# mLSTM scores from fp32r parts instead of fp32, and the second parts of three weight pieces made on GpSimd

## The chip, the cores and the metric

The kernel runs on one core of a Trainium2 chip. The metric is device time in microseconds (us) of one execution: the median of three runs before the change is 978.38 us.

## The reference, cut to what matters

Two post-norm layers: half-step SwiGLU FFN, token mixing, half-step SwiGLU FFN, each followed by a LayerNorm, on 256 positions of width 1024. The mixer of the second layer is an mLSTM of four heads of width 192 beside a cross-attention into 256 memory tokens. Of the mLSTM the part that matters here is:

```python
qk = jax.nn.silu(causal_dwconv(qk, qk_conv_w))     # width 4, over positions
q, k = jnp.split(qk, 2, -1)                        # 768 = 4 heads x 192 each
...
sc = jnp.einsum('bhtd,bhsd->bhts', q_, k_) * w_intra
num = (jnp.einsum('bhts,bhse->bhte', sc, v_) + ...)
den = jnp.sum(sc, -1) + ...
h = num / jnp.maximum(jnp.abs(den), jnp.exp(-m_t))[..., None]
```

The kernel computes the chunked recurrence as one causal 256 x 256 matrix of scores for each head, weighted by a decay matrix. Everything is asked for in fp32.

## The kernel before, in words

**Exact parts.** An fp32 value x is split into h, x rounded to fp32r, and l = x - h, also fp32r. `split` (L107) does it: ScalarE (ACT) copies into h (L108), VectorE (DVE) subtracts (L109). A product of two values is then three fp32r matmuls: h by h, h by l, l by h. Nearly all matmuls of the kernel are such products; a few are in plain fp32, among them the mLSTM scores and the sums over values (`numer`).

**Weights.** The weights are listed as pieces in the order of their use (`pieces`), each 1 MB or less. `trace_piece` (L118) loads a piece into a `raw` tile (three buffers) by a DMA on the queue of SP (L138) and splits it, 1024 columns at a time, into `wh` and `wl` (five buffers each). `get` (L146) runs one piece ahead of use. A raw buffer is free for the next DMA when both parts have been made from it, and a wh and wl buffer when the matmuls have read it. The dictionary `behind` puts a piece's split, on the engine concerned, behind a given instruction.

The pieces of the mLSTM stage are, in order of use (their number follows in the names of the order's rows): wm 0 (122) for the queries of the cross-attention; wv 0,0 and 0,1 (123, 124) for the values of heads 0 and 1; wm 1 (125), wm 4 (126), wm 2 (127), wm 5 (128); wv 1,0 and 1,1 (129, 130) for the values of heads 2 and 3; wm 3 (131), wm 6 (132); four pieces of the output projection (133 to 136); then the gate and up weights of the last FFN (137 on). wm 1 to 3 make k, wm 4 to 6 make q, 256 channels each.

**The mLSTM stage**, `mlstm_mixer`, in the order in which TensorE (PE) runs it from L809 on. `qk_piece` (L718) projects 256 channels (tiles qkp, two banks of 128 channels, 24 products each, L457 to L459), applies the convolution from the bank (one ACT and three DVE instructions for each 128 channels, L724 and L726) into a tile qr, and then the SiLU of 512 columns on ACT (L730) into a tile `qk`. Names such as qr01 mean which = 0 (q; 1 is k) and i = 1. PE does k0 and q0 (i = 0), with the cross-attention's scores between them; in the middle of q0 come the matmuls `negm` that spread a row over the partitions, from which DVE (L708) and ACT (L709, L711) make the four decay matrices, in buffers named kT, vm, og and decay (`decay`, L698). Then k1 with the transposes pT of the softmax in its middle (L520), q1, the values of heads 2 and 3 (tile v), the outputs of the cross-attention (xo, L530), the scores of heads 0 and 1 (`mscores(0)`, tiles ms), k2 with `numer` in its middle, q2, the first parts of the output projection (yo), the scores of heads 2 and 3 (`mscores(1)`), and the rest.

**mscores** (L735). The 768 channels lie in six chunks of 128 partitions. Each head has one whole chunk (`al`) and half of another (`lo` or `hi`, 64 partitions), by the table HP. For each of two row tiles of positions (256 columns, then 128, because of the causal triangle) it does the whole chunks, as two matmuls of 64 output columns each (`mm_halves`, L209), then the half chunks (L746), one head's beside the other's.

**Banks.** PSUM has two rings of four banks. The ring of `ybank` holds, in this stage and in this order: the scores of the cross-attention (4), negm of heads 0 and 1, negm of heads 2 and 3, pT (4), v (2), xo (2), ms of heads 0 and 1. So the fourth pT takes the bank of the second negm.

**Order.** The instructions of each engine stand in a fixed order that a scheduler makes from the program when it is built; an engine runs them in that order.

Of the kernel before, what the change touches and what calls it, by code (L numbers as in the profile page):

```python
# [8 lines left out]
F32 = mybir.dt.float32  # L9
F32R = mybir.dt.float32r  # L10
AF = mybir.ActivationFunctionType
# [3 lines left out]
P = 128  # L15
T = 256
# [15 lines left out]
def trunk(ctx: ExitStack, tc: tile.TileContext, d, out):  # L32
    nc = tc.nc
    pe, act, dve, pool = nc.tensor, nc.scalar, nc.vector, nc.gpsimd
# [5 lines left out]
    hp = ctx.enter_context(tc.tile_pool(name="hp", bufs=5))  # L40
# [7 lines left out]
    def ybank(name):  # L48
        return psy.tile([P, 512], F32, tag="y", name=name)
# [45 lines left out]

    state = {"next": 0, "used": 0}
    made = {}
    behind = {}

    def after(*ins):  # L100

        stack = ExitStack()
        for i in ins:
            stack.enter_context(tc.issue_after(i))
        return stack

    def split(raw, h, l):  # L107
        act.activation(h, raw, AF.Copy)  # L108
        dve.tensor_sub(l, raw, h.bitcast(F32))  # L109

    def new_act(name):

        return actp.tile([P, KC, 2, T], F32R, tag="a", name=name)

    def split_act(raw, a, k0, n):
        split(raw.rearrange("p (k t) -> p k t", k=n), a[:, k0:k0 + n, 0], a[:, k0:k0 + n, 1])

    def trace_piece(first=False):  # L118
        n = state["next"]
        if n >= len(pieces):  # L120
            return
        key, src, width = pieces[n]
        state["next"] = n + 1
        if not first:
            raw = rawp.tile([P, 2048], F32, tag="raw", name=f"raw{n}")
        if key == ("mem",):
            nc.sync.dma_start(raw, src)
            made[key] = new_act("memT")
            for q in range(2):
                split_act(raw[:, 1024 * q:1024 * q + 1024], made[key], 4 * q, 4)  # L130
            return
        h = wp.tile([P, 2048], F32R, tag="wh", name=f"wh{n}")
        l = wp.tile([P, 2048], F32R, tag="wl", name=f"wl{n}")
        made[key] = (h, l)
        if first:
            return h, l
        if n >= 6:
            nc.sync.dma_start(raw[:, :width], src)  # L138
        for c in range(0, width, SPLIT):
            s = slice(c, min(c + SPLIT, width))  # L140
            if n < 6:
                nc.sync.dma_start(raw[:, s], src[:, s])
            with after(*behind.get(key, ())):
                split(raw[:, s], h[:, s], l[:, s])

    def get(*key):  # L146
        while state["next"] < len(pieces) and state["next"] <= state["used"] + 1:
# [12 lines left out]
    first = [trace_piece(first=True) for _ in range(2)]  # L160
# [7 lines left out]
    for k in range(KC):  # L168
        q, o = (k, 0) if k < 2 else (1 + k // 2, k % 2 * CH)
        nc.sync.dma_start(xw[q][:, o:o + CH], d["xw"][:, k * CH:(k + 1) * CH])  # L170
        h, l = first[k // 4]
        s = slice((k % 4) * 512, (k % 4) * 512 + 512)
# [33 lines left out]
    def mm_halves(o, a, b, start, stop):  # L206

        for m in HALVES:
            pe.matmul(o[m], a[:, m], b, start=start, stop=stop)  # L209

    def tsl(t):
        return slice(t * P, (t + 1) * P)
# [397 lines left out]
    lo, hi, al = slice(0, 64), slice(64, 128), slice(0, 128)  # L610
    HP = [((0, al), (1, lo)), ((1, hi), (2, al)), ((3, al), (4, lo)), ((4, hi), (5, al))]

    def mlstm_mixer(mix, i):
# [7 lines left out]
        for t in range(2):  # L621
            banks = [ybank(f"op{t}{h}") for h in range(2)]
            for k in range(KC):
                for h in range(2):
                    n = 392 if h else 384
                    s = slice((k % 2) * 776 + 384 * h, (k % 2) * 776 + 384 * h + n)
# [21 lines left out]
        li, f, e, u = [rows[0][:NH, n, :] for n in range(4)]  # L648
# [6 lines left out]
        mask = kv[0][:, 384:]  # L655
# [42 lines left out]
        def decay():  # L698
            nb = {h: ybank(f"negm{h}") for h in (0, 2)}
            o = [nb[h // 2 * 2][:, h % 2 * T:h % 2 * T + T] for h in range(NH)]  # L700
            for h in range(NH):
                for n in range(2):
                    pe.matmul(o[h], pick[:, h:h + 1].to_broadcast([P, P]), eh[:, n], start=n == 0,
                              stop=n == 1)
            for h in range(NH):
                Et = E[h]
                for t in range(2):
                    m = dve.tensor_add(Et[:, 256 * t:256 * t + P], o[h][:, tsl(t)], mask)  # L708
                    act.activation(Et[:, 256 * t:256 * t + P], Et[:, 256 * t:256 * t + P], AF.Exp,  # L709
                                   bias=cols[:, t, h:h + 1])  # L710
                last = act.activation(Et[:, P:256], o[h][:, P:], AF.Exp, bias=cols[:, 0, h:h + 1])  # L711
            behind["wm", 5] = behind["wv", 1, 0] = (m.ins,)
            return last.ins


        qk = [hp.tile([P, 2, 2, T], F32, tag="h", name=f"qk{n}") for n in range(3)]

        def qk_piece(which, i, mid=None):  # L718
            r = tmp(f"qr{which}{i}")

            def use(c, b):
                o = c * 256
                w = [qcw[:, 6 * which + 2 * i + c, q:q + 1] for q in range(4)]
                act.activation(r[:, o:o + 256], b, AF.Copy, scale=w[3])  # L724
                for q, sh in ((0, 3), (1, 2), (2, 1)):
                    dve.scalar_tensor_tensor(r[:, o + sh:o + 256], b[:, :256 - sh], w[q],  # L726
                                             r[:, o + sh:o + 256], op0=ALU.mult, op1=ALU.add)

            proj_direct(get("wm", (1 if which else 4) + i), f"qkp{which}{i}", use, mid)
            return lambda: act.activation(qk[i][:, which].rearrange("p c t -> p (c t)"), r, AF.Silu)  # L730

        def qkc(c, which, r, s):
            return qk[c // 2][r, which, c % 2, s]

        def mscores(a):  # L735
            hs = (2 * a, 2 * a + 1)
            b = {h: (ybank if a == 0 else mbank)(f"ms{h}") for h in hs}
            for s in range(2):
                ts_ = slice(0, 256) if s == 0 else slice(P, 256)
                o = {h: b[h][:, 0:256] if s == 0 else b[h][:, 256:384] for h in hs}  # L740
                for h in hs:
                    c = next(c for c, r in HP[h] if r is al)
                    mm_halves(o[h], qkc(c, 1, al, tsl(s)), qkc(c, 0, al, ts_), True, False)
                for h in hs:
                    c, r = next((c, r) for c, r in HP[h] if r is not al)
                    pe.matmul(o[h], qkc(c, 1, r, tsl(s)), qkc(c, 0, r, ts_), start=False, stop=True)  # L746
            for h in hs:
                dve.scalar_tensor_tensor(E[h][:, :384], b[h][:, :384], DH ** -0.5, E[h][:, :384],
                                         op0=ALU.mult, op1=ALU.mult)
# [66 lines left out]
        ends = []  # L816
# [9 lines left out]
        xa.values(1)  # L826
        mscores(0)
        qk_piece(1, 2, lambda: (numer(0, 0), numer(1, 0)))()
        qk_piece(0, 2)()
        o = OutProj(1, mix, i)  # L830
        tokens(0, 0)
        tokens(1, 0)
# [25 lines left out]
    mix = new_act("mix0")  # L858
# [11 lines left out]
    o = OutProj(0, mix, 1)  # L870
# [63 lines left out]
```

## Time and profile before

| what | value |
|---|---|
| median of 3 runs | 978.38 us (978.30 to 978.86) |
| the profiled execution, whole | 978.59 us |
| its span, first to last instruction | 976.2 us |
| granted clock of TensorE, mean | 0.999 |
| the mLSTM stage from k0 to the end of the second scores | about 700 to 764 us of the span |
| GpSimd (POOL) busy, over the span | 20.5 us in 32 instructions |
| HBM read | 185.01 MB |

The profile is of one execution. A row of its timeline gives the start in us from the span's start, the duration, the engine, the line of the kernel, the operation, out<-in, the shapes, and how many like instructions in a row it stands for; PE is a matmul, PEld the load of its weights. A matmul's recorded duration includes its way through the array, so the pace of matmuls is read from start to start, not from durations. A plain fp32 matmul of the program shows as two records, an fp32r matmul as one. Where idle time stood before an instruction, the row ends with it and with what ended it; "issue" means that nothing in the profile held it.

### The profile page before, as it was taken

What the parts mean: (1) busy time and instruction counts of PE and PEld (TensorE: products, weight loads), DVE (VectorE), ACT (ScalarE), POOL (GpSimd) and SP (SyncE); (2) the same over time, 40 slices, a digit from 0 to 9 for tenths busy, and PEclk for the clock granted to TensorE, in tenths of its full rate; (3) what the DMA queues carried; (4) which work ended last, traced back from release to release, by engine and by line L of the source; (5) the groups of instructions that cost most, each with busy time, mean ns of one, the idle gap of its engine ahead of it and who ended that gap; (6) DMA issues with size and microseconds to landing.
All of it is one profiled execution on the core that took longest, in us unless ns stands there. A gap on an engine that the chain in (4) does not pass through costs nothing.

```text
span 976.2 us, 13253 instructions
## 1 busy us (share of the span) xinstructions
PE 967.2 (99%) x5266; PEld 831.0 (85%) x5266; DVE 662.9 (68%) x1016; ACT 527.1 (54%) x847; POOL 20.5 (2%) x32
## 2 busy tenths in 40 slices
PE   9999999999999999999999999999999999999997
PEld 8888888888888888888888888889999788888885
DVE  7685657869667755656875656568698786565565
ACT  7565555447535545555444555545885345555540
POOL 0000000000000000000000000001000000000000
PEclk9999999999999999999999999999999999999999
DMA  9784645566444654646375464633645446546421
GB/s 327 282 305 165 218 170 207 178 224 216 168 173 176 241 200 160 218 170 214 131 278 196 151 234 139 233 124 108 237 148 215 167 175 246 202 147 226 159 87 43
DMA packets 28142, 186.91 MB, mean 191 GB/s; under 512 B 3505, under 2 KB 3505, under 8 KB 7217
## 3 DMA queue, kind: packets, MB, share of 16 engines
q1 hardware_dynamic: 27792, 185.55, 52.6%
q8 instruction: 41, 0.67, 0.3%
q10 hardware_dynamic: 288, 0.52, 0.1%
q14 instruction: 21, 0.16, 0.0%
HBM read 185.01 MB, written 1.05 MB: 191 GB/s over the span
## 4 chain that ended last, share of the span: by engine, by line
PE 97%; DMA 1%; DVE 1%; ACT 0%; issue 0%; SPq 0%; DVEq 0%; ACTq 0%
PE gu L197 43%; PE y L189 8%; PE y L191 8%; PE y L190 8%; PE gx L191 2%; PE gx L189 2%; PE gx L190 2%; PE cx L197 2%; PE cb L197 2%; PE cg L197 2%; PE yo L189 2%; PE yo L191 2%; PE yo L190 1%; PE qkp L457 1%; PE qkp L458 1%; PE qkp L459 1%
## 5 line engine op out<-in xcount | busy, mean ns | idle before, releaser
L109 DVE TENSOR_TENSOR wl<-raw,wh 128x1024 fp32r<-128x1024 f32 x334 | 394.2, 1206 | 139.9 <-ACT wh L108 139.0
L108 ACT ACTIVATE wh<-raw 128x1024 fp32r<-128x1024 f32 x334 | 333.0, 1043 | 125.3 <-PE y L191 63.2
L197 PE MATMUL gu<-x,wh 128*128 128x512 f32 x1216 | 388.9, 395 | 0.2
L197 PEld LDWEIGHTS gu<-x,wl 128*128 128x128 f32 x1216 | 228.3, 188 | 52.2 <-DVE wl L109 0.8
L197 PE MATMUL gu<-x,wl 128*128 128x256 f32 x1216 | 242.8, 278 | 0.3 <-DVE wl L109 0.2
L197 PEld LDWEIGHTS gu<-x,wh 128*128 128x128 f32 x1216 | 189.5, 189 | 4.0 <-ACT wh L108 0.6
L189 PE MATMUL y<-wh,h 128*128 128x512 f32 (+1 forms) x352 | 137.4, 390 | 0.0
L190 PE MATMUL y<-wl,h 128*128 128x512 f32 (+1 forms) x352 | 136.6, 388 | 0.0
L191 PE MATMUL y<-wh,h 128*128 128x512 f32 (+1 forms) x352 | 136.5, 389 | 0.0
L202 DVE TENSOR_TENSOR s<-s,gu 128x256 f32<-128x256 f32 x152 | 63.0, 417 | 103.8 <-ACT s L201 103.6
L201 ACT ACTIVATE s<-gu 128x256 f32<-128x256 f32 x152 | 57.9, 382 | 105.7 <-PE gu L197 105.7
L191 PEld LDWEIGHTS y<-wh,h 128*128 128x128 f32 x352 | 66.1, 188 | 14.2 <-DVE h L334 0.4
L190 PEld LDWEIGHTS y<-wl,h 128*128 128x128 f32 x352 | 66.1, 188 | 13.6
L189 PEld LDWEIGHTS y<-wh,h 128*128 128x128 f32 x352 | 66.1, 188 | 12.9 <-ACT h L333 0.7
L333 ACT ACTIVATE h<-s 128x256 fp32r<-128x256 f32 x76 | 31.8, 418 | 66.1 <-DVE s L330 66.1
L329 ACT ACTIVATE s<-s 128x256 f32<-128x256 f32 x76 | 31.6, 416 | 37.6 <-DVE s L202 37.6
L334 DVE TENSOR_TENSOR h<-s,h 128x256 fp32r<-128x256 f32 x76 | 32.0, 421 | 17.3 <-ACT h L333 17.1
L189 PE MATMUL gx<-wh,x 128*128 128x512 f32 x96 | 38.0, 396 | 0.0
L191 PE MATMUL gx<-wh,x 128*128 128x512 f32 x96 | 37.6, 392 | 0.0
L190 PE MATMUL gx<-wl,x 128*128 128x512 f32 x96 | 37.4, 390 | 0.0
L330 DVE SCALAR_TENSOR_TENSOR s<-s 128x256 f32<-128x256 f32 x76 | 32.0, 421 | 1.7 <-ACT s L329 0.4
L457 PE MATMUL qkp<-x,wh 128*128 128x256 f32 x96 | 27.5, 287 | 0.0
(223 smaller groups left out, 967.6 us busy)
## 6 DMA issues: line engine op xcount, KB each, us to landing
raw<-in_wgu SPq DMA_DIRECT2D x83, 1024.0 KB, 4.8
raw<-in_wd SPq DMA_DIRECT2D x43, 1024.0 KB, 4.8
raw<-in_wconv SPq DMA_DIRECT2D x10, 1024.0 KB, 4.8
raw<-in_wout SPq DMA_DIRECT2D x8, 1024.0 KB, 4.8
raw<-in_wm SPq DMA_DIRECT2D x7, 1024.0 KB, 5.0
gb<-in_lngb SPq DMA_DIRECT2D x6, 1024.0 KB, 4.6
raw<-in_wkv SPq DMA_DIRECT2D x4, 1024.0 KB, 4.9
raw<-in_wop SPq DMA_DIRECT2D x4, 776.0 KB, 4.3
```

Of the source, the lines that this page charges most:

```text
L108: act.activation(h, raw, AF.Copy)
L109: dve.tensor_sub(l, raw, h.bitcast(F32))
L189: pe.matmul(o, ah, bh, start=start, stop=False)
L190: pe.matmul(o, ah, bl, start=False, stop=False)
L191: pe.matmul(o, al, bh, start=False, stop=stop)
L197: pe.matmul(o, w[part], b, start=(k, part) == (0, 0), stop=(k, part) == (KC - 1, 0))
L201: act.activation(o, bank[:, T:], AF.Copy)
L202: dve.tensor_add(o, o, bank[:, :T])
L330: dve.scalar_tensor_tensor(t_[:, 256:], t_[:, :256], 0.5, t_[:, 256:], op0=ALU.mult, op1=ALU.mult)
L333: act.activation(hh, t_[:, 256:], AF.Copy)
L334: dve.tensor_sub(hT[g][:, 1, fc, :], t_[:, 256:], hh.bitcast(F32))
L457: pe.matmul(o, w[0][:, s], a[:, 0], start=k == 0, stop=False)
```

## The change

The scores take q and k as exact parts. After the SiLU, which now writes back into qr, each 128 channels are split by `split` into h and l. The parts of chunks 0 to 2 go into the tile `mix`, the mixer's output, whose first six chunks receive no outputs before those scores are done; those of chunks 3 to 5 go into three tiles that take the place of `qk`. `mscores` does each product as three fp32r matmuls, the whole chunks with all 128 output columns at once, the half chunks alternating between the two heads.

The second parts of the pieces wm 5, wv 1,0 and wv 1,1 are subtracted on POOL instead of DVE, and no longer wait for the last addition of `decay`. The split of the first gate piece of the last FFN is put behind the split of q2.

```diff
+    aside = {("wm", 5), ("wv", 1, 0), ("wv", 1, 1)}
...
-    def split(raw, h, l):
-        act.activation(h, raw, AF.Copy)
-        dve.tensor_sub(l, raw, h.bitcast(F32))
+    def split(raw, h, l, eng=None):
+        first = act.activation(h, raw, AF.Copy).ins
+        return first, (eng or dve).tensor_sub(l, raw, h.bitcast(F32)).ins
...
-                split(raw[:, s], h[:, s], l[:, s])
+                split(raw[:, s], h[:, s], l[:, s], pool if key in aside else None)
...
-            behind["wm", 5] = behind["wv", 1, 0] = (m.ins,)
...
-        qk = [hp.tile([P, 2, 2, T], F32, tag="h", name=f"qk{n}") for n in range(3)]
+        late_qk = [hp.tile([P, 2, 2, T], F32R, tag="h", name=f"qk{n}") for n in range(3)]
+
+        def qk(c, which):
+            return mix[:, 2 * c + which] if c < 3 else late_qk[c - 3][:, which]
...
-            return lambda: act.activation(qk[i][:, which].rearrange("p c t -> p (c t)"), r, AF.Silu)
+            def done():
+                act.activation(r, r, AF.Silu)
+                for c in range(2):
+                    o = qk(2 * i + c, which)
+                    ends = split(r[:, c * T:(c + 1) * T], o[:, 0], o[:, 1])
+                return ends
+            return done
...
+                def products(h, whole, n):
+                    c, r = next((c, r) for c, r in HP[h] if (r is al) == whole)
+                    k, q = ((0, 0), (0, 1), (1, 0))[n]
+                    pe.matmul(o[h], qk(c, 1)[r, k, tsl(s)], qk(c, 0)[r, q, ts_],
+                              start=whole and n == 0, stop=not whole and n == 2)
                 for h in hs:
-                    c = next(c for c, r in HP[h] if r is al)
-                    mm_halves(o[h], qkc(c, 1, al, tsl(s)), qkc(c, 0, al, ts_), True, False)
-                for h in hs:
-                    c, r = next((c, r) for c, r in HP[h] if r is not al)
-                    pe.matmul(o[h], qkc(c, 1, r, tsl(s)), qkc(c, 0, r, ts_), start=False, stop=True)
+                    for n in range(3):
+                        products(h, True, n)
+                for n in range(3):
+                    for h in hs:
+                        products(h, False, n)
...
-        qk_piece(0, 2)()
+        behind["gu", 1, 1, 0, 0] = qk_piece(0, 2)()
```

The change adds lines, so a line of the changed kernel has a number higher by one in the upper part (L108 is L109 there). Three places in the order of the instructions show what moves. The first is ACT while the decay matrices are made, before the change; wh131 is the first part of wm 3, og and decay the last two decay matrices, negm2 the bank that they are read from:

```order
L709 ACTIVATE og_5796<-og_5796,cols_5867 128x128
L724 ACTIVATE qr00_6140<-qkp00_1_6208,qcw_169 128x256
L709 ACTIVATE vm0_1750<-vm0_1750,cols_5867 128x128 x2
L711 ACTIVATE vm0_1750<-negm0_6178,cols_5867 128x128
L711 ACTIVATE og_5796<-negm2_6179,cols_5867 128x128
L709 ACTIVATE decay3_5862<-decay3_5862,cols_5867 128x128 x2
L711 ACTIVATE decay3_5862<-negm2_6179,cols_5867 128x128
L730 ACT_TABLE_LOAD
```

The same place on ACT now:

```order
L109 ACTIVATE wh131_6424<-raw131_6423 128x1024
L710 ACTIVATE vm0_1750<-vm0_1750,cols_5867 128x128 x2
L712 ACTIVATE vm0_1750<-negm0_6178,cols_5867 128x128
L710 ACTIVATE og_5796<-og_5796,cols_5867 128x128
L712 ACTIVATE og_5796<-negm2_6179,cols_5867 128x128
L728 ACTIVATE qr00_6140<-qkp00_1_6208,qcw_169 128x256
L109 ACTIVATE wh131_6424<-raw131_6423 128x1024
L710 ACTIVATE decay3_5862<-decay3_5862,cols_5867 128x128 x2
L712 ACTIVATE decay3_5862<-negm2_6179,cols_5867 128x128
L736 ACT_TABLE_LOAD
```

Both halves of wh131, which stood behind the SiLU of k0 and q0, now stand ahead of the last decay matrix.

The second place is PE in the middle of k1, where the four softmax tiles are transposed. Before:

```order
L520 MATMUL pT1_10_6289<-ident_162,p1_10_6114 128x128 x4
L520 MATMUL pT1_11_6295<-ident_162,p1_11_6124 128x128 x4
L457 MATMUL qkp11_1_6301<-x3_5553,wh127_6142 128x256
L458 MATMUL qkp11_1_6301<-x3_5553,wh127_6142 128x256
L459 MATMUL qkp11_1_6301<-x3_5553,wl127_6143 128x256
```

And now:

```order
L521 MATMUL pT1_10_6297<-ident_162,p1_10_6114 128x128 x4
L458 MATMUL qkp11_1_6309<-x3_5553,wh127_6142 128x256
L459 MATMUL qkp11_1_6309<-x3_5553,wh127_6142 128x256
L460 MATMUL qkp11_1_6309<-x3_5553,wl127_6143 128x256
L521 MATMUL pT1_11_6303<-ident_162,p1_11_6124 128x128 x4
```

Three products of k1 have moved ahead of the fourth group of transposes.

The third place is PE at the first scores, which follow the cross-attention's outputs xo and read the tile qk before:

```order
L530 MATMUL xo1_1_6474<-p1_11_6124,vm1_1752 64x256 x2
L209 MATMUL ms0_6481<-qk0_5869 64x256 x2
L209 MATMUL ms1_6482<-qk1_5870 64x256 x2
L746 MATMUL ms0_6481<-qk0_5869 128x256
L746 MATMUL ms1_6482<-qk0_5869 128x256
```

And now the tile mix:

```order
L531 MATMUL xo1_1_6490<-p1_11_6124,vm1_1752 64x256 x2
L753 MATMUL ms0_6497<-mix1_5696 128x256 x3
L753 MATMUL ms1_6498<-mix1_5696 128x256 x3
L753 MATMUL ms0_6497<-mix1_5696 128x256
L753 MATMUL ms1_6498<-mix1_5696 128x256
```

Six fp32 matmuls, each two records in the profile, have become twelve of fp32r, since the last two rows come three times; then both repeat all of it with 128 columns.

More of the change, by code (lines that the diff above doesn't have):

```diff
@@ L707, in decay @@
                 for t in range(2):
-                    m = dve.tensor_add(Et[:, 256 * t:256 * t + P], o[h][:, tsl(t)], mask)
+                    dve.tensor_add(Et[:, 256 * t:256 * t + P], o[h][:, tsl(t)], mask)
                     act.activation(Et[:, 256 * t:256 * t + P], Et[:, 256 * t:256 * t + P], AF.Exp,
@@ L729, in qk_piece @@
             proj_direct(get("wm", (1 if which else 4) + i), f"qkp{which}{i}", use, mid)
-            return lambda: act.activation(qk[i][:, which].rearrange("p c t -> p (c t)"), r, AF.Silu)
-        def qkc(c, which, r, s):
-            return qk[c // 2][r, which, c % 2, s]
+            def done():
[5 more added lines that the diff above has]
+            return done
         def mscores(a):
```

## The prediction

> **What bounds the kernel now.** I read the page first, then who waited on PE's weight side in the stage that the change touches, then PE's timeline around the two score groups. The page:
>
> ```profile
> PE 967.2 (99%) x5266; PEld 831.0 (85%) x5266; DVE 662.9 (68%) x1016; ACT 527.1 (54%) x847; POOL 20.5 (2%) x32
> PE 97%; DMA 1%; DVE 1%; ACT 0%; issue 0%; SPq 0%; DVEq 0%; ACTq 0%
> ```
>
> PE is busy for 99% of the span and carries 97% of the chain that ended last. Whether that holds in this stage too, the waits of PE's weight loads between 690 and 782 us say (longest first; these are the first four):
>
> ```profile
> PEld ms L746 <- issue: 1.1, 4, 0.4
> PEld ms L209 <- issue: 1.0, 3, 0.4
> PEld num L209 <- issue: 0.4, 1, 0.4
> PEld cols L691 <- DVE qr L726: 0.3, 1, 0.3
> ```
>
> The largest wait for another engine is 0.3 us. So relieving DVE can return almost nothing; the time changes by what PE itself gains or loses, and by waits that are new.
>
> **The scores' own time.** PE's timeline, first score group, then the products of k2 that follow:
>
> ```profile
> 738.62 1.08 PE L209 MATMUL ms<-qk 128*64 128x256 f32 x8
> 739.63 0.70 PE L746 MATMUL ms<-qk 64*128 64x256 f32 x4
> 740.26 0.66 PE L209 MATMUL ms<-qk 128*64 128x128 f32 x8
> 740.85 0.49 PE L746 MATMUL ms<-qk 64*128 64x128 f32 x4
> 741.27 0.39 PE L457 MATMUL qkp<-x,wh 128*128 128x256 f32 x1
> 741.49 0.28 PE L458 MATMUL qkp<-x,wh 128*128 128x256 f32 x1
> 741.61 0.28 PE L459 MATMUL qkp<-x,wl 128*128 128x256 f32 x1
> ```
>
> Second group, between products of the output projection:
>
> ```profile
> 761.08 0.39 PE L191 MATMUL yo<-wh,mix 128*128 128x512 f32 x1
> 761.39 1.08 PE L209 MATMUL ms<-qk 128*64 128x256 f32 x8
> 762.41 0.70 PE L746 MATMUL ms<-qk 64*128 64x256 f32 x4
> 763.04 0.66 PE L209 MATMUL ms<-qk 128*64 128x128 f32 x8
> 763.63 0.49 PE L746 MATMUL ms<-qk 64*128 64x128 f32 x4
> 764.05 0.50 PE L189 MATMUL yo<-wh,mix 128*128 128x512 f32 x1
> 764.39 0.39 PE L190 MATMUL yo<-wl,mix 128*128 128x512 f32 x1
> 764.62 0.39 PE L191 MATMUL yo<-wh,mix 128*128 128x512 f32 x1
> ```
>
> Start to start, the four L746 records take 0.63 us with 256 columns and 0.42 with 128. They run as two pairs, one head's half chunk beside the other's, so the 0.21 us between them is 2 x 128 columns: 0.82 ns a column in fp32, and 0.21 us is left that does not depend on the columns. That is the price of changing the shape in which the array is used (64*128, 128*64, 128*128) and of the first weights. The eight L209 records (four pairs of 64 output columns) give the same: 1.02 in the second group against 0.59 is 0.84 ns a column, with 0.16 us left.
>
> An fp32r product of 256 columns takes 0.12 us (741.49 to 741.61), one of 512 columns 0.23 (764.39 to 764.62): 0.43 ns a column, half the fp32 pace, and an fp32r product is one record where fp32 needs two. On paper that is 3 x 0.43 = 1.3 ns a column for three products against 2 x 0.83 = 1.7. But each product loads its weights anew:
>
> ```profile
> 741.27 0.19 PEld L457 LDWEIGHTS qkp<-x,wh 128*128 128x128 f32 x1
> 741.38 0.19 PEld L458 LDWEIGHTS qkp<-x,wh 128*128 128x128 f32 x1
> ```
>
> Two loads of 128 columns with nothing in front start 0.11 us apart. At 256 moving columns the load is just hidden; at 128 it should set the pace.
>
> **The sum for PE.** Each group becomes 24 records, as before: six whole products of 256 columns, three pairs of half ones, six of 128 columns, three pairs. I take 0.12 us a slot for all 18: 2.16 us, plus 0.21 for each change of shape.
>
> - First group: it follows 64-column matmuls, so there are five changes (the last to k2): 2.16 + 1.05 = 3.21. Before, from 738.62 to full pace (741.49 less 0.12), 2.75. So +0.46.
> - Second group: the products in front have its shape, so four changes: 2.16 + 0.84 = 3.00. Before, from 761.08 + 0.23 to 764.39 - 0.23, 2.85. So +0.15.
>
> Together +0.6. The uncertain price is the 18 slots of 128 columns, since no fp32r matmul under 256 columns is in this trace. From below, the line through 0.12 and 0.23 gives 0.07 a slot, so 18 x 0.05 = 0.9 less, in sum -0.3. From above, the fp32 price for such a product, two passes of 128 columns at 0.82 ns, is 0.21: 18 x 0.09 = 1.6 more, in sum +2.2. I take 0.12, from the nearest row: same operation, same weights, and a load pace of 0.11 that is its floor.
>
> The Trainium skill (TensorE: Matmul & The Clock Gate, Back-to-back issue gap) has about 81 ns for each matmul of 128 columns in a stream of loads and matmuls. By it the 18 slots would cost 0.7 us less and the sum would be about -0.1; the load pace of 0.11 us in this trace speaks against that here.
>
> **ACT and the decay matrices: the new wait.** ACT before, from a row that shows two wh copies in 1.99 us on:
>
> ```profile
> 700.43 1.99 ACT L108 ACTIVATE wh<-raw 128x1024 fp32r<-128x1024 f32 x2
> 715.54 0.46 ACT L724 ACTIVATE qr<-qkp,qcw 128x256 f32<-128x256 f32 x1
> 715.90 0.68 ACT L709 ACTIVATE vm<-vm,cols 128x128 f32<-128x128 f32 x2
> 717.84 0.70 ACT L709 ACTIVATE decay<-decay,cols 128x128 f32<-128x128 f32 x2 [0.46 <-DVE decay L708]
> 718.44 0.35 ACT L711 ACTIVATE decay<-negm,cols 128x128 f32<-128x128 f32 x1
> ```
>
> The last of these ends at 718.79 and frees the second negm bank. PE's transposes before:
>
> ```profile
> 718.04 1.91 PE L520 MATMUL pT<-ident,p 128*128 128x128 f32 x16
> 719.71 0.36 PE L457 MATMUL qkp<-x,wh 128*128 128x256 f32 x1
> ```
>
> They are 0.104 us apart, so the fourth group, which takes that bank, began at 719.29, half a microsecond behind its release. In the order of the change both halves of wh131 stand ahead of the last decay matrix. They can run there, because the raw buffer is now free early: POOL subtracts wm 5 at once, where DVE held it until the rows below, and its DMA followed at 720.33.
>
> ```profile
> 717.92 4.09 DVE L109 TENSOR_TENSOR wl<-raw,wh 128x1024 fp32r<-128x1024 f32 x4
> 725.14 0.68 DVE L109 TENSOR_TENSOR wl<-raw,wh 128x512 fp32r<-128x512 f32 x1
> 720.33 0.33 SPq L138 DMA_DIRECT2D raw<-in_wm  x1
> raw<-in_wm SPq DMA_DIRECT2D x6, 1024.0 KB, 5.3
> 679.15 1.85 POOL L637 TENSOR_TENSOR og<-og,hnb 128x768 f32<-128x768 f32 x1 [6.35 <-ACT og L636]
> ```
>
> The chain is then: 715.54 + 0.99 (wh131) + 1.40 (vm to og, 715.90 to about 717.30) + 0.36 (qr) + 0.99 (wh131) + 0.60 + 0.35 (decay) = 720.23, 1.4 later. PE has three products more ahead of the fourth pT group, 0.36 us and some 0.08 for the return to transposes and back, so it arrives at 719.73 and waits 0.5. With the 0.08 that is **+0.6**. It could be nothing, if the copies find gaps that I don't see, or 1 us more, if wh131's data comes a microsecond late. Queued behind it on PE is everything, since PE runs in order.
>
> **POOL.** 1.85 us for 768 columns is 2.4 ns a column: 2.5 us for 1024, 1.2 for 512, so 4 x 2.5 + 2 x 1.2 = 12.4 us, beginning at 701.4 behind the first copy of wm 5. wm 5 is done at 706.4, its raw buffer refilled by 711.7 (5.3 us to landing), ahead of 715.54. All is done by 714; PE wants wm 5 in q1, from 719.71 + 24 x 0.12 = 722.6 on, and the values 5.8 us later.
>
> **The extra splits.** Twelve copies and twelve subtractions of 256 columns, priced by the same shapes in the FFN:
>
> ```profile
> L333 ACT ACTIVATE h<-s 128x256 fp32r<-128x256 f32 x76 | 31.8, 418 | 66.1 <-DVE s L330 66.1
> L334 DVE TENSOR_TENSOR h<-s,h 128x256 fp32r<-128x256 f32 x76 | 32.0, 421 | 17.3 <-ACT h L333 17.1
> 734.06 0.62 ACT L730 ACTIVATE qk<-qr 128x512 f32<-128x512 f32 x1
> 759.78 0.64 ACT L730 ACTIVATE qk<-qr 128x512 f32<-128x512 f32 x1 [1.38 <-DVE qr L726]
> ```
>
> ACT gets 12 x 0.42 = 5.0 us more. DVE gets 5.0 more and loses 5.9 of wl: the 4.09 and 0.68 quoted, and one more of 1024 columns at (4.09 - 0.68) / 3 = 1.14. Their cover: q1's SiLU ended at 734.7, 3.9 us before PE needs it at 738.62; the two copies, a subtraction and the 1.4 us of delay on ACT take some 2.5 of that. q2's SiLU ended at 760.4, 1.0 before 761.39; the parts take 1.1 more, but the wh and wl of the next FFN's first piece, about 1 us each, now stand behind them, and PE reads q2's chunk only in the second head's turn, 0.36 us into the group. I cost both at nothing; without that cover the second would cost up to 0.3 us. That FFN piece is late by some 3 us and is read a LayerNorm later.
>
> **Sum.** 978.59 (the profiled execution) + 0.6 + 0.6 = 979.8. It stood 0.2 above the median of the runs, so against 978.38 I predict **979.6 us**. A measurement of this kernel can tell about 0.2% (2.0 us) from no change: that is no change.
>
> **The rivals.**
>
> - *Narrow fp32r products at the fp32 price, slower.* If 128 moving columns cost 0.21 us in fp32r, each group's 128-column half costs 9 x 0.09 us more: +1.6, in all +2.8, 981.2. It decides once a slot costs over 0.16 us. For it: every fp32r product in this trace has 256 columns or more, so nothing shows the contrary. Against: 0.43 ns a column at 256 and at 512. 24%.
> - *The half chunks don't run in pairs in fp32r.* 12 more slots of 0.12 us: +1.4, 981.0. Against: the four fp32 records in 0.63 us, in the same row halves. 5%.
> - *POOL is slower beside DVE.* The one row that prices it tells nothing of DVE beside it. If 1024 columns took over 4.4 us ((715.5 - 5.3 - 701.4) / 2), raw131 would land late, hold ACT in front of the decay matrices, and PE with it; at twice the price the landing is at 716.6, +1.1, 980.7. 8%. The Trainium skill (GPSIMD Engine Reference, Specifications) says that GpSimd shares its SBUF interfaces with VectorE and contends with instructions of two SBUF inputs there; no run here shows it yet.
> - *Faster.* It needs 2 us out of groups that take 5.6 us in all; the floor above, 0.07 a slot and no new wait, gives -0.3 (978.1), and the waits for other engines hold no more than a few tenths. 3% for what I overlook.
> - *As forecast, within 0.2%*, the floor included: 60%.
>
> Slower by over 0.2% then has 24 + 5 + 8 = 37%, within it 60%, faster 3%. The range goes from 978.0 (the floor) to 981.8 (the dear narrow products with 0.6 us more of waiting).
>
> **What would show it.** In the changed profile: the 128-column ms rows at 0.11 to 0.13 us a product; ms groups of about 3.2 and 3.0 us; a wait of PE before the last pT, released by ACT's decay, near 719.7; POOL's wl rows at 2.5 us, ended by 714; no wait of PE for mix or qk. I am wrong if the narrow products cost 0.2, if PE waits in front of either score group, or if the time falls by more than 1 us.

## The result, and the profile after

| | before | after |
|---|---|---|
| median of 6 runs each | 978.34 us (978.18 to 978.86) | 984.41 us (983.30 to 985.38) |
| ratio, with its 95% interval | | 1.0061 (1.0050 to 1.0072) |
| the profiled execution, its span | 978.59, 976.2 us | 985.38, 983.6 us |
| GpSimd (POOL) busy | 20.5 us | 32.8 us |

The kernel became 6.1 us slower. The forecast was 979.6 us, and its range ended at 981.8. In the page of after PE holds 93% of the chain that ended last in place of 97%; DVE, ACT and DMA have the rest.

```profile
PE 969.5 (99%) x5266; PEld 834.5 (85%) x5266; DVE 667.2 (68%) x1022; ACT 530.0 (54%) x859; POOL 32.8 (3%) x38
PE 93%; DVE 3%; ACT 2%; DMA 2%; issue 0%; DVEq 0%; SPq 0%; ACTq 0%
```

PE's own waits for other engines between 690 and 782 us, where the same view of before is empty (columns: us in total, times, the longest):

```profile
PE negm L704 <- ACT p L507: 2.2, 2, 2.0
PE pT L521 <- ACT decay L712: 1.7, 1, 1.7
PE pT L521 <- ACT vm L712: 0.9, 1, 0.9
```

The forecast had one wait of 0.5 us, at the fourth pT, and none at negm. A negm bank held scores of the cross-attention before, and the softmax on ACT (tile p) frees it. PE at negm, before and after:

```profile
711.37 1.07 PE L703 MATMUL negm<-eh,pick 128*128 128x256 f32 x8
713.19 0.70 PE L704 MATMUL negm<-eh,pick 128*128 128x256 f32 x4 [1.97 <-ACT p L507]
```

On ACT the softmax stands behind eh, and eh waits for the end of the row computation on DVE, so the next view to read is DVE's timeline there. After, with the first two scalings of the softmax as its last row:

```profile
701.60 2.45 DVE L679 TENSOR_TENSOR rows<-rows 4x256 f32<-4x256 f32 x1
704.08 2.77 DVE L680 TENSOR_TENSOR_SCAN rows<-rows 4x256 f32<-4x256 f32 x1
...
713.99 2.13 DVE L512 TENSOR_SCALAR p<-p,ri 128x256 f32<-128x256 f32 x2
```

Before, the same three (one line number lower):

```profile
701.79 0.41 DVE L678 TENSOR_TENSOR rows<-rows 4x256 f32<-4x256 f32 x1
702.24 0.68 DVE L679 TENSOR_TENSOR_SCAN rows<-rows 4x256 f32<-4x256 f32 x1
...
710.62 0.61 DVE L511 TENSOR_SCALAR p<-p,ri 128x256 f32<-128x256 f32 x2
```

Two instructions on a tile of 4 x 256 values took 2.45 and 2.77 us in place of 0.41 and 0.68: 4.1 us more. POOL's timeline in the same microseconds:

```profile
701.35 4.95 POOL L110 TENSOR_TENSOR wl<-raw,wh 128x1024 fp32r<-128x1024 f32 x2 [12.91 <-ACT wh L109]
708.70 7.28 POOL L110 TENSOR_TENSOR wl<-raw,wh 128x1024 fp32r<-128x1024 f32 x4 [2.39 <-ACT wh L109]
```

POOL did two subtractions from 701.35 to 706.30, as fast as forecast (2.48 us each). DVE's two instructions lie over them, and each ends just behind one of them. The two scalings lie over the last two of POOL's other four, which end at 715.98. What that did to ACT, which runs in order:

```profile
707.26 0.42 ACT L683 ACTIVATE eh<-rows 4x256 fp32r<-4x256 f32 x1 [4.66 <-DVE rows L681]
...
712.07 0.47 ACT L507 ACTIVATE p<-sc,nm 128x256 f32<-128x256 f32 x1 [0.74 <-DVE nm L502]
...
716.88 0.48 ACT L507 ACTIVATE p<-sc,nm 128x256 f32<-128x256 f32 x1 [1.75 <-DVE nm L502]
...
720.44 1.04 ACT L109 ACTIVATE wh<-raw 128x1024 fp32r<-128x1024 f32 x1
...
723.12 1.05 ACT L109 ACTIVATE wh<-raw 128x1024 fp32r<-128x1024 f32 x1
...
724.65 0.36 ACT L712 ACTIVATE decay<-negm,cols 128x128 f32<-128x128 f32 x1
```

The same view of before, at eh and at the first and the last but one row of the softmax:

```profile
703.33 0.42 ACT L682 ACTIVATE eh<-rows 4x256 fp32r<-4x256 f32 x1 [0.53 <-DVE rows L680]
...
708.71 0.48 ACT L506 ACTIVATE p<-sc,nm 128x256 f32<-128x256 f32 x1 [0.63 <-DVE nm L501]
...
711.99 0.48 ACT L506 ACTIVATE p<-sc,nm 128x256 f32<-128x256 f32 x1 [0.22 <-DVE nm L501]
```

ACT waited for DVE at eh and at the softmax already, so the rows had no slack there. Now it stands for 4.66 us at eh, and everything behind it (the copies of wv, the convolution of k0, the softmax) is late: the first softmax row by 3.4 us. The stretched scalings, through the maxima that follow them on DVE, make ACT's wait at the last but one row 1.75 us in place of 0.22, so that this row is 4.9 us late. The last decay matrix ends at 725.01 in place of 718.79. The two rows of wh131 ahead of it are the copies that the prediction spoke of.

PE's third loss is in its clock. The windows of after (us, then PE's and PEld's, DVE's, ACT's and POOL's busy time; the first of the last three columns is the granted clock):

```profile
724.00:726.00 2.00, 0.94 (x6) 0.94 (x7) 1.83 (x3) 1.98 (x5) 0.00 (x0) 0.87 0.00 0
726.00:728.00 2.00, 2.00 (x12) 2.00 (x11) 0.19 (x1) 1.99 (x6) 0.00 (x0) 0.50 0.75 217
728.00:730.00 2.00, 2.00 (x15) 2.00 (x15) 1.97 (x6) 2.00 (x7) 0.00 (x0) 0.78 0.73 307
```

Right behind the wait at pT the clock is halved for (0.13 + 0.50 + 0.22) x 2 / 0.50 = 3.4 us, which costs 1.7 us. Before, it was 1.00 throughout this stage. Sum: 2.2 at negm, 2.6 at pT, 1.7 of clock make 6.5, of the 6.8 us between the two profiled executions (7.4 between their spans). The rest is not accounted for.

The scores themselves, in PE's timeline, each group with the row that shows its end:

```profile
745.68 2.81 PE L753 MATMUL ms<-mix 128*128 128x256 f32 x24
...
748.65 0.28 PE L459 MATMUL qkp<-x,wh 128*128 128x256 f32 x1
...
768.46 2.72 PE L753 MATMUL ms<-qk 128*128 128x256 f32 x24
...
771.44 0.39 PE L191 MATMUL yo<-wl,mix 128*128 128x512 f32 x1
```

Measured as the prediction measured them, the first group takes 748.65 - 0.12 - 745.68 = 2.85 us (before 2.75), the second 771.44 - 0.23 - 768.46 = 2.75 (before 2.85). In sum nothing.

### The profile page after: what moved, and what is told of

Same layout as the page of the kernel before. It is cut to its first block, busy times and chain, and to the rows that moved or that the text cites. A ratio compares the mean times of both kernels' runs of the same rounds, so it can differ in the third digit from the quotient of the medians.

```text
span 983.6 us, 13290 instructions
## 1 busy us (share of the span) xinstructions
PE 969.5 (99%) x5266; PEld 834.5 (85%) x5266; DVE 667.2 (68%) x1022; ACT 530.0 (54%) x859; POOL 32.8 (3%) x38
## 3 DMA queue, kind: packets, MB, share of 16 engines
HBM read 185.01 MB, written 1.05 MB: 189 GB/s over the span
## 4 chain that ended last, share of the span: by engine, by line
PE 93%; DVE 3%; ACT 2%; DMA 2%; issue 0%; DVEq 0%; SPq 0%; ACTq 0%
PE gu L198 43%; PE y L190 8%; PE y L192 8%; PE y L191 8%; PE gx L192 2%; PE gx L190 2%; PE gx L191 2%; PE cx L198 2%; PE cb L198 2%; PE cg L198 2%; PE yo L190 2%; PE yo L192 1%; PE yo L191 1%; PE kb L198 1%; DMA raw<-in_wm 1%; ACT wh L109 1%
## 5 line engine op out<-in xcount | busy, mean ns | idle before, releaser
L110 DVE TENSOR_TENSOR wl<-raw,wh 128x1024 fp32r<-128x1024 f32 x328 | 388.1, 1209 | 139.3 <-ACT wh L109 138.4
L109 ACT ACTIVATE wh<-raw 128x1024 fp32r<-128x1024 f32 x334 | 332.8, 1043 | 122.4 <-PE y L192 59.7
```

Of the source, the lines that this page charges most:

```text
L109: first = act.activation(h, raw, AF.Copy).ins
L110: return first, (eng or dve).tensor_sub(l, raw, h.bitcast(F32)).ins
```

## The experiments

**The theory, and its rivals.** Theory 1: a GpSimd instruction on SBUF (the memory that both engines read and write) stops, for its whole length, those DVE instructions that need the same access to it. The row computation is such a chain and has no slack, so ACT, negm, the decay matrices and pT follow. Theory 2: the extra splits and products cost the time. Theory 3: the order on ACT (the copies of wm 3, wh131, ahead of the last decay matrix; two of the expectations name wm 5 for it) costs it.

**One half of the change alone.** e1_scores_only takes POOL out:

```diff
-    aside = {("wm", 5), ("wv", 1, 0), ("wv", 1, 1)}
+    aside = set()
...
-                    dve.tensor_add(Et[:, 256 * t:256 * t + P], o[h][:, tsl(t)], mask)
+                    m = dve.tensor_add(Et[:, 256 * t:256 * t + P], o[h][:, tsl(t)], mask)
...
+            behind["wm", 5] = behind["wv", 1, 0] = (m.ins,)
```

> The changed kernel with the second parts of the three pieces back on DVE, behind the last mask addition, as in the kernel before; the scores stay three products of two parts. Theory 1 (the subtractions on GpSimd stop DVE instructions that share its access to SBUF; that delays the rows, the softmax, the decay matrices and so PE): nearly all of the loss is gone, 978.5 to 979.2 us, which is the score products alone (0.24 us in the first group by the trace of after, some 0.2 in the second), no wait of PE ahead of negm or pT over 0.5 us. Theory 2 (the split of q and k and the score products cost it): still 983 us or more. Theory 3 (ACT's order, two copies of wm piece 5 ahead of the last decay matrix, costs it): the copies now wait no less than in the kernel before, so this run cannot tell it from theory 1, but it stays under 980.

Measured: 978.29 us against 978.55 of before beside it, ratio 0.9997 (0.9989 to 1.0006). PE is busy throughout at full clock from 690 to 764 us; two of the windows, in the columns of above:

```profile
690.00:718.00 28.00, 28.00 (x210) 27.17 (x210) 23.86 (x59) 24.69 (x54) 0.00 (x0) 1.00 0.36 133
718.00:738.00 20.00, 20.00 (x150) 19.43 (x150) 19.80 (x32) 17.72 (x33) 0.00 (x0) 1.00 0.67 238
```

The scores as three products, with all their splits, cost nothing that this can measure. Theory 2 falls. Theories 1 and 3 are not parted, since the copies of wh131 come behind the decay matrices here.

e2_pool_only is the other half: the fp32 scores and `qk` tiles of before, with `aside` and its argument to `split` as in the change.

> The kernel before (its fp32 scores) with the second parts of the three pieces on GpSimd and nothing held back behind the mask additions: the other half of the change alone. Theory 1: 983 to 985 us, rows chain stretched (0.41 to about 2.4 us for one subtraction, 0.68 to about 2.7 for one scan), a wait of PE of about 2 us at negm and about 3 us at pT, and a granted clock under 1.00 in the stretch after the waits. Theory 2: within 1 us of 978.4. Theory 3: the copies of wm5 stand ahead of the decay exponentials here too, so some 2 us of the wait at pT would stay if DVE were not stopped: 980 to 981.

Measured: 984.86 us, ratio 1.0064 (1.0049 to 1.0080). The rows are stretched to 2.45 and 2.77 us as in after, the waits are 2.0 at negm and 2.6 at pT, and the clock is halved for 3.4 us behind them. The whole loss is in the three pieces on GpSimd.

**Which of the six subtractions.** If theory 1 is right, it matters what DVE does beside them and not how many they are. e11_only_wm5_on_pool and e10_only_wv_on_pool part the set; what is taken out goes back to DVE, behind the last mask addition. First e11, then e10:

```diff
-    aside = {("wm", 5), ("wv", 1, 0), ("wv", 1, 1)}
+    aside = {("wm", 5)}
...
+            behind["wv", 1, 0] = (m.ins,)
```

```diff
-    aside = {("wm", 5), ("wv", 1, 0), ("wv", 1, 1)}
+    aside = {("wv", 1, 0), ("wv", 1, 1)}
...
+            behind["wm", 5] = (m.ins,)
```

> The changed kernel with only wm 5 on GpSimd (two subtractions, at about 701 to 706 us), the wv pieces back on DVE behind the mask additions. Theory 1: the rows chain is stretched as in the changed kernel and eh comes 4 us late, so the softmax on ACT comes late; its scaling then meets no GpSimd instruction: a wait at negm of 0.5 to 2 us and some at pT, 980 to 983 us. If the subtractions cost by their number (two of six): 980.5 at most.

> The changed kernel with only the two wv pieces on GpSimd, wm 5 back on DVE behind the mask additions. GpSimd then begins at about 705 us, when the rows have left DVE. Theory 1: the rows are not stretched and eh is as early as before; only the scaling of the softmax rows (SBUF to SBUF) is held off, and the maxima behind it on DVE: a wait of PE at negm of 0.5 to 2 us, 979 to 981.5 us. If the subtractions cost by their number (four of six are left): 982.5 or more.

Measured: two subtractions, 982.29 us, ratio 1.0040 (1.0024 to 1.0056); the other four, 978.87 us, ratio 1.0003 (0.9994 to 1.0013). DVE's timeline with the two:

```profile
701.69 2.45 DVE L679 TENSOR_TENSOR rows<-rows 4x256 f32<-4x256 f32 x1
704.18 2.78 DVE L680 TENSOR_TENSOR_SCAN rows<-rows 4x256 f32<-4x256 f32 x1
```

With the four, which POOL does from 703.86 to 711.10, DVE's timeline reads:

```profile
700.88 0.41 DVE L679 TENSOR_TENSOR rows<-rows 4x256 f32<-4x256 f32 x1
701.32 0.68 DVE L680 TENSOR_TENSOR_SCAN rows<-rows 4x256 f32<-4x256 f32 x1
...
704.69 1.52 DVE L731 SCALAR_TENSOR_TENSOR qr<-qkp,qcw,qr 128x253 f32<-128x253 f32 x3 [1.42 <-ACT qr L729]
...
709.62 0.67 DVE L502 TENSOR_REDUCE nm<-sc 128x2 f32<-128x512 f32 x1
710.21 1.30 DVE L512 TENSOR_SCALAR p<-p,ri 128x256 f32<-128x256 f32 x2
```

That is the selection in one view. The shifts (one input in PSUM, 0.48 us each) and the maxima (from PSUM, 0.67) run at their usual pace in the middle of POOL's work; only the first scaling (SBUF to SBUF) waits, until POOL ends at 711.10. PE never waits, so the wait at negm that the expectation of e10 had does not come. The harm, then, begins with the first two subtractions. That e11 stands 2 us under after, though it has the same stretched rows, fits its smaller waits: 1.5 us at negm (where PE also came 0.9 us later than in after), 1.2 at pT, and no drop of the clock in its profile. Its scaling meets no GpSimd instruction. These waits make 2.7 of its 4.0 us; the rest is open.

The two runs differ in a second thing: both copies of wh131 stand ahead of the last decay matrix in e11 and behind it in e10. Only e6 below takes these copies away and leaves POOL's work where it is; it still loses 4.6 us, so the copies are not the whole cause.

**Later, or in smaller pieces.** e3_pool_gated holds the subtractions until the softmax is through DVE:

```diff
             k0()
             q0()
+        gate = pool.tensor_copy(bg[:, :1], xa.p[1, 1][:, 511:])
+        behind["wm", 5] = behind["wv", 1, 0] = (gate.ins,)
```

> The changed kernel with a copy of one column on GpSimd, which reads the last scaled softmax tile, ahead of the six subtractions on GpSimd: they begin at about 714 us where the rows and softmax are through DVE, rather than at 701. Theory 1: the rows chain and negm go back to the times of before; what is left is the score products and whatever the subtractions stop on DVE after 714 (mask additions, the k1 and q1 shifts): 978.6 to 980.5 us. Theory 2: 983 or more. Theory 3 (order on ACT): the copies still stand ahead of the decay exponentials, so a wait of 1 to 2 us at pT stays: 980 to 981.

Measured: 984.85 us, ratio 1.0066 (1.0053 to 1.0079). The number is missed, and so is what the expectation says of theory 3: the copies of wh131 come behind the decay matrices here. Theory 1 is borne out by what DVE does beside POOL. POOL and DVE, one timeline each:

```profile
714.37 12.36 POOL L110 TENSOR_TENSOR wl<-raw,wh 128x1024 fp32r<-128x1024 f32 x6
```

```profile
714.48 0.28 DVE L709 TENSOR_TENSOR kT<-negm,kT 128x128 f32<-128x128 f32 x1
...
721.74 5.60 DVE L110 TENSOR_TENSOR mix<-qr,mix 128x256 fp32r<-128x256 f32 x4 [3.59 <-ACT mix L109]
```

The waits at negm and pT are gone. The mask additions (bank and mask) keep their 0.28 us beside POOL, but the four subtractions for the parts of k0 and q0, which read SBUF twice, take 5.60 us in place of 4 x 0.42. ACT waits for them and for late loads (1.7 us for one of them), and PE then waits 1.9 us ahead of the scores for ACT's copy of v. Behind that wait the clock is halved for 10 us, which is 5 us of the loss:

```profile
739.00:742.00 3.00, 1.07 (x5) 0.73 (x5) 3.00 (x3) 2.96 (x7) 0.00 (x0) 0.96 0.97 355
742.00:752.00 10.00, 9.81 (x46) 8.61 (x46) 4.79 (x9) 2.01 (x3) 0.00 (x0) 0.50 0.75 297
```

e8_pool_gated_fp32_scores puts the same gate into e2_pool_only, so that DVE has no parts of q and k to make there.

> The kernel before with its fp32 scores and the same six subtractions on GpSimd from 714 us on, behind the one-column copy of e3_pool_gated. DVE then has no second parts of q and k to make between 714 and 727 us; what it does there (mask additions, shifts) reads PSUM and one SBUF tile. Theory 1: no DVE instruction is stretched by more than its own wait for the next gap, no wait of PE over 0.5 us, clock 1.00: 978.0 to 979.0 us, so the same GpSimd work costs nothing there and 6.5 us twelve microseconds earlier. If GpSimd work costs in itself: 980 or more.

Measured: 979.12 us (978.34 to 980.89), ratio 1.0012 (1.0004 to 1.0021). The same six subtractions cost 0.7 us in place of 6.3, as theory 1 has it, though the time lies just above the expected range and one wait of PE was not expected. (The copies of wh131 come behind the decay matrices here too.) The one DVE instruction with two SBUF inputs that falls on them is stretched again (first row), and the price of POOL's slower pace shows as well: the buffers come free late, so ACT stands waiting for a load (second), and its copy of v releases PE late. The profiled execution, 1.7 us over the median, shows that wait (third). DVE, ACT and PE:

```profile
725.01 2.37 DVE L110 TENSOR_TENSOR wl<-raw,wh 128x1024 fp32r<-128x1024 f32 x1
```

```profile
733.79 1.06 ACT L109 ACTIVATE wh<-raw 128x1024 fp32r<-128x1024 f32 x1 [3.38 <-DMA raw<-in_wout]
```

```profile
741.08 0.65 PE L210 MATMUL ms<-qk 128*64 128x256 f32 x4 [1.71 <-ACT v L799]
```

A wait of 1.7 us at the very place where e3 had one of 1.9; here the clock stays at 1.00.

e4_pool_256 keeps after's place and cuts each subtraction into pieces:

```diff
+        if eng is not None:
+            for c in range(0, raw.shape[1], 256):
+                e = slice(c, c + 256)
+                eng.tensor_sub(l[:, e], raw[:, e], h[:, e].bitcast(F32))
+            return
```

> The changed kernel with each subtraction on GpSimd cut into pieces of 256 columns: same work, same start, but each instruction holds for about 0.65 us in place of 2.48. Theory 1, if DVE gets in between two GpSimd instructions: no DVE instruction is stretched by more than about 0.7 us, and the wait at negm shrinks from 2 us to about 1: 980.5 to 983 us. If GpSimd keeps its access from one instruction to the next the time stays at 984 or more. Theories 2 and 3: no change, 984 to 985.

Measured: 983.38 us, ratio 1.0051 (1.0037 to 1.0065). DVE, then POOL:

```profile
701.88 0.79 DVE L684 TENSOR_TENSOR rows<-rows 4x256 f32<-4x256 f32 x1
702.70 1.11 DVE L685 TENSOR_TENSOR_SCAN rows<-rows 4x256 f32<-4x256 f32 x1
```

```profile
701.64 15.24 POOL L113 TENSOR_TENSOR wl<-raw,wh 128x256 fp32r<-128x256 f32 x20 [13.14 <-ACT wh L109]
```

DVE does get in between two pieces, and no row is stretched by more than 0.54 us, but now all five from there to eh are. POOL's total grows from 12.2 to 15.2 us, and its end from 716.0 to 716.9. The negm wait is gone altogether, but 3.6 us are lost at the third and fourth pT, with the clock halved for 6.8 us from the first of these two waits on; so the time lies just above the expected range.

**One input in place of two.** e5_pool_one_input leaves the subtraction out and copies the piece in its place:

```diff
+        if eng is not None:
+            return first, eng.tensor_copy(l, raw).ins
```

> The changed kernel with each of GpSimd's six subtractions replaced by a copy of the raw piece (one tensor input in place of two; the second parts of the three pieces are then wrong, since the subtraction is left out). Theory 1a (any GpSimd instruction that reads and writes SBUF holds off DVE's two-input and SBUF-to-SBUF instructions for its length): the same DVE instructions are stretched, but for the length of the copy, which is shorter if GpSimd takes one input faster than two (about 1 us in place of 2.4): 980 to 983 us. Theory 1b (only two-input GpSimd instructions do it): no stretched DVE instruction, 978.3 to 979.

Measured: 979.79 us, ratio 1.0016 (1.0006 to 1.0025). DVE, then POOL:

```profile
700.44 1.14 DVE L678 TENSOR_TENSOR rows<-rows,rows 4x256 f32<-4x256 f32 x1
701.62 1.42 DVE L680 TENSOR_TENSOR_SCAN rows<-rows 4x256 f32<-4x256 f32 x1
```

```profile
698.03 5.42 POOL L111 CAST wl<-raw 128x1024 fp32r<-128x1024 f32 x4 [9.53 <-PE v L193]
```

Theory 1a holds, with a time just under its range: a copy stops DVE too. It is 1.2 us long in place of 2.5 and needs no wait for ACT's part, so it does less harm by length and by place; the two are not parted here. This run also shows the other side: the first copy begins 0.03 us behind a DVE subtraction of 1024 columns, which keeps its 1.23 us, and the copy takes 2.11 us. So it is the one that begins second that waits.

**The order on ACT.** e6_copies_behind_decay:

```diff
+        behind["wm", 3] = (ends[0],)
         with tc.issue_after(ends[0]):
```

> The changed kernel with ACT's two copies of piece wm 3 held behind the last decay exponential. Theory 1 with the order on ACT as a second part: the wait at negm stays at 2 us, the decay ends about 2 us earlier (723 in place of 725), the wait at pT falls from 2.7 to about 1, and the granted clock may stay up: 981 to 983 us. Theory 1 alone (the copies only fill time in which ACT waits for DVE anyway): no change, 984 to 985.

Measured: 982.97 us, ratio 1.0049 (1.0035 to 1.0063). The decay ends at 723.15 in place of 725.01, as theory 3 has it for its share, and PE waits 1.5 us in place of 2.2 at negm and 0.3 in place of 2.6 at pT. The intervals of e6 and after overlap, so the median difference of 1.4 us is no more than a hint. Part of the gain at pT went back: in this execution the clock was halved behind the wait at negm, for 3.4 us, and PE came to pT later. Theory 3 alone falls: without the copies 4.6 us stay.

**The clock.** Does the drop come from the wait in front of it? e7_dummies_in_waits and e12_dummies_own_bank fill the two waits at pT with products that nobody reads; e9_k1_fills_wait fills them with real ones, by moving the last two pT tiles behind the second half of k1.

In `turns`, ahead of pT tile n, e12 has

```diff
+                for _ in range((0, 0, 7, 16)[n] if self.l else 0):
+                    with tc.issue_after(last):
+                        last = pe.matmul(spare, cur["x"][:, 0, 0, :P], cur["x"][:, 0, 0], start=True, stop=True).ins
```

with `spare` a bank of its own; e7 has the same with weights and x of k1, and the unused half of k1's bank. And e9:

```diff
-        qk_piece(1, 1, xa.turns)()
+        k1 = qk_piece(1, 1, lambda: first_turns.append(xa.turns(slice(0, 2))))
+        xa.turns(slice(2, 4), lastp[0])
+        k1()
```

> The changed kernel with 7 and 16 products that nobody reads (weights and x of the k projection, into the unused half of its bank) ahead of the third and the fourth pT tile, where TensorE waits 0.95 and 2.3 us; the wait of 2 us ahead of negm stays as it is. If the low granted clock (0.50 from 725.5 to 728.8 us) comes from TensorE's idle time: no drop, and 1.6 us less than the changed kernel, 982.5 to 983.2 us, though more work is done. If it comes from something else, or from the earlier wait at negm: 984.2 to 985.

> As e7_dummies_in_waits, which met a wait of 8 us on its own bank: now the 7 and 16 products that nobody reads go to a bank of their own. If the low granted clock after the waits at pT comes from TensorE's idle time: no drop behind pT, and 1.6 us less than the changed kernel, 982.5 to 983.2 us (a drop behind the wait at negm, as e6_copies_behind_decay showed one, may take its place: then 984 to 985). If it comes from something else: 984.2 to 985 with the drop where it was.

> The changed kernel with the last two pT tiles moved behind the second half of the k projection (24 products, 2.9 us), so that TensorE has work while ACT finishes the decay matrices. If the low clock comes from TensorE's idle time before the drop: the wait at pT goes from 2.7 us to under 1, no drop after it, 980 to 981.5 us; a drop after the earlier wait at negm may stay, and then 981.5 to 982.5. If the time is set by something further on (softmax parts, scores waiting for DVE): 983.5 or more.

Measured: e7 994.75 us, ratio 1.0173 (1.0159 to 1.0187). It tells nothing of the question, since the added products themselves waited 7.8 us, for DVE to finish reading the other half of their bank. e12 984.95, ratio 1.0064 (1.0046 to 1.0082). e9 982.10, ratio 1.0036 (1.0023 to 1.0050). In e12's timeline PE has no gap at pT:

```profile
724.32 1.08 PE L526 MATMUL spare<-x 128*128 128x256 f32 x7
725.24 0.60 PE L530 MATMUL pT<-ident,p 128*128 128x128 f32 x4
725.59 2.15 PE L526 MATMUL spare<-x 128*128 128x256 f32 x16
```

Behind it the clock is 1.00 in both e12 and e9, but in both it was halved earlier, behind the wait at negm (0.50 in e12 from 716 to 719 us), where after's was not. So the drop went where a wait was left, as the second case of both expectations has it. (In these two profiles PE had one more wait before it, of 1.0 and 0.7 us for the rows, which came late.) That fits a cause in PE's idle time, and does not settle it, since other profiles have waits of 1.2 to 1.7 us and no drop (e11, e8, e5), and after has none behind its 2.0 at negm. Between 704 and 764 us the halved stretches of all profiles are 3.4 us long (after, e2, e6, e9, e12) or about 6.8 (e4) or 10.2 (e3); e7 has one of 3.4 and one of 10.2.

The Trainium skill (TensorE: Matmul & The Clock Gate, What's actually happening) has the gate judge PE's activity in windows of 3.4 us that run freely. The lengths here agree: one, two and three of them. It has the drop after at least one idle window of that length, while here it came behind waits of 1.5 us (e6) and 1.9 us (e3); if the waits are its cause, a shorter one can do it.

## Why the prediction was wrong, point by point

- *The failed step is "POOL"*: the 12.4 us of subtractions were priced (12.2 measured, wm 5 done at 706.3 against 706.4 forecast) and counted as hidden because POOL was idle, with only POOL's own users asked after. What DVE does beside them was never asked. In the runs the first two stretched DVE's rows by 4.1 us, and the kernel with them alone lost 4.0 of the 6.1 us (e11, the early copies of wh131 included); the other four alone cost nothing that was measured (e10), and add to the loss only behind the first two, where they also stretch the scaling. POOL's work ended at 715.98 in place of 714, since it waited 2.4 us for ACT's late copies.
- *The rival on contention had the wrong side.* It let POOL be slowed by DVE and set the threshold at 4.4 us for 1024 columns. POOL took 2.5; DVE was stopped, because POOL began first (where DVE did, in e5, POOL was stopped). The Trainium skill (SBUF — State Buffer, Who interferes with whom) says whichever of the two begins first holds the shared access for its whole instruction, and names a DVE instruction with two SBUF inputs and a GpSimd instruction that reads SBUF. The traces agree for L679 and L680 (2.45 and 2.77 us), and for what it leaves free: the shifts and mask additions with one input in PSUM keep 0.48 and 0.28 us. By an estimate from that rule and POOL's 2.5 us, the two rows would have been forecast at about 2.5 us each.
- *The rows had no slack, and this stood in the profile before.* ACT waited 0.53 us for DVE ahead of eh and 0.63 ahead of the first softmax row. The prediction asked whether relieving DVE returns anything, and found that it doesn't (e10 and e8 relieve it and gain nothing); it did not ask what stopping DVE costs. An engine busy for 68% of the span can still be the one that a stage waits for.
- *The wait at pT: right in place, and in part in mechanism; too small.* Forecast 0.5 us at the fourth pT, measured 1.7 there and 0.9 at the third. The two copies stand there with 1.04 and 1.05 us, as forecast. But they came on top of a softmax that ended 4.9 us late (its last ACT row at 717.34 against 712.45), and what hid them in the sum, half a microsecond of slack, was gone already. No run has the early copies with the rows on time, so their own 0.5 us is not measured.
- *The clock was not in the sum.* 1.7 us in after's profile; the forecast held waits to their own length.
- *The scores: right that narrow fp32r products go at the pace of the weight load.* +0.6 was forecast and 0.0 measured. Each group's 24 records fit 18 slots of 0.115 us, so the changes of shape took in the mean (2.85 - 2.07) / 5 = 0.16 us each in the first group and (2.75 - 2.07) / 4 = 0.17 in the second, in place of the 0.21 read from fp32 rows. The rest of the +0.6 was the slot, 0.12 where the starts of the records lie 0.11 (128 columns) to 0.12 us (256) apart, 0.115 in the mean. The rivals on a dear narrow product and on half chunks that do not pair are both refuted by these two groups.
- *The extra splits hidden: right.* e1 has all of them and the time of before.

## What to carry to other kernels

Before work is moved to an idle engine, list what the other engines do in the same microseconds and which access to memory they share with it: here a DVE instruction that reads SBUF twice stood still to the end of a GpSimd instruction on SBUF that began before it, however small the DVE one was (2.45 us in place of 0.41). So GpSimd gets such work beside DVE instructions that read PSUM, not beside a chain that another engine waits for: the same six subtractions cost 6.3 us (e2) or 0.7 (e8). And a wait of TensorE of about 2 us can bring a fall of the clock behind it, which cost 1.7 us in after and 5 in e3.

## What the runs showed of the hardware that was not expected

- Against a GpSimd subtraction of 1024 columns (2.4 to 2.6 us): a DVE subtraction of 4 x 256 took 2.45 in place of 0.41 us, a scan 2.77 in place of 0.68, two scalings SBUF to SBUF with one tensor input up to 2.13 together in place of 0.61. DVE instructions with an input in PSUM were not stretched at all (0.48 us for a shift, 0.28 for a mask addition, with and without).
- Between two GpSimd instructions a DVE instruction gets through (e4: five rows stretched by 0.37 to 0.54 us each), so cutting the GpSimd work trades one long stop for a short one in every DVE instruction of the kind, and lengthens the GpSimd work by a quarter (15.2 against 12.2 us).
- A GpSimd copy with one input does the same for its 1.2 us, and is itself held (2.11 us) when a DVE subtraction begins just before it.
- The clock of TensorE was halved for 10 us behind a wait of 1.9 us in one profile (5 us lost), and not at all behind one of 1.7 us at the same place in another. What decides it stays open.
